# Pool projection ahead of the in-projection, its moving averages one per token tile inside the in-projection, memory keys and values behind it

## The chip, the cores and the metric

The kernel runs on one core of a Trainium2 chip. The core has a matmul engine (TensorE, PE in the profile; its weight loads are PEld), a vector engine (VectorE, DVE), an activation engine (ScalarE, ACT), a general engine (GpSimd, POOL) and a queue engine that mostly issues DMAs (SyncE, SP). Each engine works through its own instructions in order; semaphores tie them together. The metric is the time of one execution on the device in microseconds (us), the median of a few runs. Lower is better.

## The reference, cut to what matters

One layer, batch 1, 2048 tokens (S) of width 1024 (D), all in float32:

```python
xn = rmsnorm(h, g_mix)
z = einsum('bsd,dc->bsc', xn, w_in)            # q 512 | k 512 | v 512 | p_in 512 | f_logit 8
q, k = rmsnorm per head of 64 (8 heads)
fox  = forgetting_attention(q, k, v, f_logit + b_forget)   # causal, cumulated log-sigmoid of f_logit as bias
pool = multiscale_pool(p_in, w_pool, pool_scale)           # 4 groups of 128 channels: mean over the last
                                                           # 2, 4, 8, 16 tokens minus the token, a 128x128 map, a scale
h = h + concat(fox, pool) @ w_out
hn = rmsnorm(h, g_mem_q); mn = rmsnorm(mem, g_mem_kv)      # mem: 256 tokens
mq, mk, mv from hn @ w_mem_q and mn @ w_mem_kv             # 4 heads of 128
h = h + softmax(mq mk^T / sqrt(128)) mv @ w_mem_out
h = h + swiglu(rmsnorm(h, g_ffn))
```

## The kernel before, in words

Every float32 matmul of a projection is made of three: each operand is split into a rounded high part and the low rest, and `mm3` (lines 58 to 62) multiplies high by high, high by low and low by high. So wherever a tile of activations or weights enters a projection, ACT makes the high part (a copy or a scaled copy, lines 157, 176, 181) and DVE the low one (lines 55, 177), two instructions of the tile's size.

The part that the change touches lies ahead of the attention and takes 460 us. All of it but the last stage is written out by hand: each engine's instructions stand in the order in which the code issues them.

1. Memory keys and values (`kv`): 16 steps of weights for 256 memory tokens, 96 matmuls of 512 columns. The loads of the x tiles and of the in-projection's weights (`load_w_in`, 8 pieces of 128 x 1544) run under it.
2. In-projection: 16 tiles of 128 tokens. `project` multiplies a tile into four PSUM banks of 386 columns (tiles `zps`, one per quarter n, 96 matmuls), `scaled` copies the four banks out on ACT (line 327), `normed_heads` splits v, writes it to DRAM, and squares q and k (line 348); DVE sums the squares per head (line 350), POOL takes the power -1/2 (`rsqrt`, lines 69 and 71), and `split_heads` (lines 358 to 363 and 55) scales and splits q and k. `to_heads` (lines 372 to 375) turns them on PE, copies them on ACT and stores them. There are four PSUM banks for `zps`, so the first quarter of tile i+1 needs the copy of the first quarter of tile i. For each pair of tiles x is squared on ACT (line 160), added up on POOL (line 162) and summed over its channels on PE against ones (`token_sums`, line 202); this gives `rstd`, the norm of each token.
3. Pool projection: 8 blocks of 256 tokens, 96 matmuls each (`zp`), the transposed way round (channels on partitions, tokens along the row). The token norms are spread over the partitions by a matmul (`stat_diag`, `stat_bcast`, line 491). `windows` scales the block on DVE, builds the means by adding shifted copies (line 516), and splits the result; `pooled` multiplies it by `w_pool`. Under it `out_sums` prepares sums of the out-projection's weights on POOL, `cumulated` makes the cumulated forget logits (tiles fe, tots, car, written to DRAM as `cd`), and `load_head` loads the first head (`qs`, `kh`, `kl` from `qkT`, `cb` from `cd`).
4. Attention: 22 score items run ahead of the first value item. A score item is two matmuls (line 715) and one DVE instruction that adds the bias and takes the row minimum (line 717); the diagonal ones need a mask from POOL (`cm`, line 706).

Of the kernel before, what the change touches and what calls it, by code (L numbers as in the profile page):

```python
# [21 lines left out]
H = 8  # L22
# [18 lines left out]
def block_kernel(ctx: ExitStack, tc: tile.TileContext, x, xT, memT, cols, rows, w_qkvf, w_p, w_pool, w_out,  # L41
# [81 lines left out]

    xstack, lstack = ExitStack(), ExitStack()
    zp = opened(lstack, "zp")
    xp = opened(xstack, "xp", side="right")

    class Slots:
# [5 lines left out]
        def take(self, dt):  # L134
            n = self.free.pop(0)
            return n, self.pl.tile(self.shape, dt, tag=f"{self.name}{n}", name=f"{self.name}{n}", bufs=1)

# [14 lines left out]
    def x_split(tiles, part=None, qs=range(4), engs={}):  # L152

        for q in qs:
            n, raw = tiles[q]
            hi = xp.tile([P, 2, B], F32R, tag="xhi", name="xhi", bufs=8)
            act.copy(hi[:], raw[:])
            if part is not None:
                sq = xp.tile([P, 2, B], F32, tag="xsq", name="xsq", bufs=2)[:] if q else part
                act.activation(sq, raw[:], AF.Square, scale=1.0 / 32.0)  # L160
                if q:
                    pool.tensor_tensor(out=part, in0=part, in1=sq, op=ALU.add)
            m, lo = xsl.take(F32R)
            sub_hi(lo[:], raw[:], hi[:], engs.get(q))
            xsl.free.append(n)
            xlow.append(m)
            tiles[q] = hi, lo
# [18 lines left out]
    whi = [None] * KD  # L186
    wlo = [None] * KD
    wph = [None] * KD
    wpl = [None] * KD
    HIS = 16  # L190

    with ExitStack() as c0:
        was = ExitStack()
        wa = opened(was, "wa", side="right")
        tpp = opened(xstack, "tpp", space=PSUM)

        def token_sums(part):

            ssp = tpp.tile([P, 2], F32, tag="ss", name="ss", bufs=1)
            for j in range(2):  # L200
                for c in range(2):
                    pe.matmul(ssp[:, j:j + 1], lhsT=part[:, c, j * P:(j + 1) * P], rhs=ones[:, 0:1], start=c == 0,
                              stop=c == 1)
            return ssp

        def token_rstd(ssp, outp):
            ms = xp.tile([P, 2], F32, tag="ms", name="ms", bufs=2)
            dve.tensor_copy(ms[:], ssp[:])
            rsqrt(outp, ms[:])


        kvs = ExitStack()
        kvp = opened(kvs, "kvp", space=PSUM)
        first = in_order(EN.DVE, EN.Activation, EN.Pool, EN.SP)
        first.__enter__()
        kv = [[kvp.tile([P, MW], F32, name=f"kv{m}{a}") for a in range(2)] for m in range(2)]
        wk = [None] * KD
        wsl = Slots(wa, [P, QKVF], "wl", KD)
        w_raw = [None] * KD

        def w_in_hi(k, dt):

            return wa.tile([P, QKVF], dt, tag=f"wh{k}", name=f"wh{k}", bufs=1)

        def load_kv(k):
            wk[k] = w_in_hi(k, F32)[:, :2 * MW]
            sp.dma_start(wk[k], w_mem_kv[k * P:(k + 1) * P, :])

        def split_kv(k):
            t_ = slab(k % 3, dt=F32R)  # L230
            hi, lo = t_[:, :2 * MW], t_[:, 2 * MW:]
            split(hi, lo, wk[k], g_mem_kv[:, k:k + 1])
            return hi, lo

        def load_w_in(k):

            n, raw = wsl.take(F32) if k < KD - 1 else (None, slab(3))
            w_raw[k] = n, raw[:, :QKVF]
            sp.dma_start(w_raw[k][1], w_qkvf[k * P:(k + 1) * P, :])

        def split_w_in(k):
            n, raw = w_raw[k]
            whi[k] = w_in_hi(k, F32R)
            wlo[k] = wsl.take(F32R)[1]
            split(whi[k][:], wlo[k][:], raw, g_mix[:, k:k + 1])
            wsl.free.append(n)

        mt = []
        for k in range(4):
            mt += x_load(0, memT.rearrange("(k p) m -> p k m", p=P), (k,))  # L250
            load_kv(k)
        xt = x_load(0)
        mpart = xp.tile([P, 2, B], F32, tag="part", name="part", bufs=1)
        mr = cst.tile([P, 2], F32, name="mr")
        for k in range(KD):
            if k < 4:
                x_split(mt, mpart[:], (k,))
            wh, wl = split_kv(k)
            mh, ml = x_part(mt, k)
            if k == 3:  # L260
                token_rstd(token_sums(mpart), mr[:])
            for m in range(2):
                ms_ = slice(m * P, (m + 1) * P)
                for a in range(2):
                    as_ = slice(a * MW, (a + 1) * MW)
                    mm3(kv[m][a][:], (mh[:, ms_], ml[:, ms_]), (wh[:, as_], wl[:, as_]), k == 0, k == KD - 1)
            if k < 4:
                load_kv(k + 4)
            if k == 1:
                load_w_in(0)  # L270
            if k == 3:
                for c in range(1, KD):
                    load_w_in(c)
            if k == 6:
                split_w_in(0)
            if k == 5:
                part = xp.tile([P, 2, B], F32, tag="part", name="part", bufs=1)
                x_split(xt, part[:])
        split_w_in(1)
        mks_ = [slab(n, dt=F32R)[:].rearrange("p (a c) -> p a c", a=2) for n in (2, 0)]  # L280
        mkv = [t_[:, a] for t_ in mks_ for a in range(2)]
        mkh, mkl = (t_.rearrange("p (h m) -> p h m", h=MH) for t_ in mkv[:2])
        mvh, mvl = (t_.rearrange("p (m c) -> p m c", m=2) for t_ in mkv[2:])
        mks, msk = ([zp.tile([P, MH, P], F32, tag="st", name="mks", bufs=4) for _ in range(2)] for _ in range(2))
        for m in range(2):
            act.activation(mks[m][:].rearrange("p h d -> p (h d)"), kv[m][0][:], AF.Copy, scale=mr[:, m:m + 1])
            split_gain(mvh[:, m], mvl[:, m], kv[m][1][:], mr[:, m:m + 1])
        for n in range(2, 4):
            sp.dma_start(mkvd[n], f(mkv[n]))
        kvs.close()  # L290

        def mem_key_norms():
            for m in range(2):
                act.activation(msk[m][:], mks[m][:], AF.Square)
                ms = zp.tile([P, MH], F32, tag="mkms", name="mkms", bufs=2)
                dve.tensor_reduce(out=ms[:], in_=msk[m][:], axis=AX.X, op=ALU.add)
                rk = zp.tile([P, MH], F32, tag="mkr", name="mkr", bufs=2)
                rsqrt(rk[:], ms[:], 1.0 / P)
                dve.tensor_tensor(out=mks[m][:], in0=mks[m][:], in1=rk[:].unsqueeze(2).to_broadcast([P, MH, P]),
                                  op=ALU.mult)  # L300
# [1384 lines left out]
```

## Time and profile before

| | |
|---|---|
| median of 3 runs | 2590.38 us (2587.77 to 2593.8) |
| profiled execution, span from first to last instruction | 2586.7 us |
| granted TensorE clock, mean | 0.994 |
| PE busy in the span | 2522.3 us (98%) |
| DVE, ACT, POOL busy | 1740.9 (67%), 1286.9 (50%), 892.2 us (34%) |
| DMA | 416.13 MB, mean 161 GB/s |

The page does not give a time of its own for the profiled execution; its span is 3.7 us under the median of the runs, and what is worked out against the span is carried over to the median by adding these 3.7 us. In the rows, "idle before <-releaser" is how long the engine stood still ahead of an instruction and which instruction of which line ended that. The duration of a matmul overlaps its neighbours, so the pace of matmuls is read from start to start.

### The profile page before, as it was taken

Reading aid. Unit: us, or ns where it says so; the run is one execution under the profiler, and the core shown is the slowest. Engines: PE = TensorE matmul, PEld = TensorE weight load, DVE = VectorE, ACT = ScalarE, POOL = GpSimd, SP = SyncE. Lnnn points to the kernel's source line nnn. Section 1 sums busy time; section 2 is a strip of 40 time slices with the busy share of each in tenths; the row PEclk is TensorE's granted clock in tenths of the full one; section 3 lists DMA queues with packets and bytes.
Section 4 is the critical chain, followed back from the end, with each engine's and each line's share of the span. In section 5 each row is a group of like instructions: output and inputs, shape, how many; then the busy total and the mean of one; then the engine's idle time right before and its main releaser. Section 6 shows DMA issues by size and latency. Waiting matters only on the chain.

```text
span 2586.7 us, 37147 instructions
## 1 busy us (share of the span) xinstructions
PE 2522.3 (98%) x13037; PEld 2169.7 (84%) x13037; DVE 1740.9 (67%) x2955; ACT 1286.9 (50%) x2444; POOL 892.2 (34%) x1185
## 2 busy tenths in 40 slices
PE   8999989999999899999999999999999999999998
PEld 7999989788888687788878888888888888888887
DVE  6444477899998755545877778756766666665554
ACT  6454443788889523555643433334543333333443
POOL 3343255445555522344425545430001222222000
PEclk9999999999999999999999999999999999999999
DMA  6443476644543545122464545447773332325665
GB/s 242 127 131 106 127 220 213 175 123 123 152 121 95 171 161 212 70 87 89 177 215 179 187 171 195 147 159 268 247 261 123 113 112 102 127 98 181 230 215 184
DMA packets 223434, 416.13 MB, mean 161 GB/s; under 512 B 26128, under 2 KB 113936, under 8 KB 212496
## 3 DMA queue, kind: packets, MB, share of 16 engines
q1 hardware_dynamic: 190800, 307.84, 37.2%
q0 software_dynamic: 32448, 105.93, 10.6%
q8 instruction: 102, 1.67, 0.3%
q14 instruction: 84, 0.69, 0.1%
HBM read 280.39 MB, written 133.30 MB: 160 GB/s over the span
## 4 chain that ended last, share of the span: by engine, by line
PE 46%; issue 8%; DVE 2%; DMA 2%; ACT 1%; POOL 1%; SPq 0%; POOLq 0%; DVEq 0%; ACTq 0%
PE bk L60 13%; PE bk L62 13%; PE bk L61 13%; PE mmps L60 2%; PE mmps L62 2%; PE mmps L61 2%; PE tp L896 1%; DMA graw<-in_w_gu_dram 1%; DVE ww L55 1%; DVE t L991 0%; DMA xraw<-hTd 0%; POOL out_dram L1578 0%; ACT mq L1069 0%; DMA hTd<-hst 0%; DVE ms L1073 0%
## 5 line engine op out<-in xcount | busy, mean ns | idle before, releaser
L55 DVE TENSOR_TENSOR ww<-draw,ww 128x512 fp32r<-128x512 f32 x308 | 205.3, 703 | 156.5 <-ACT ww L181 155.8
L181 ACT CAST ww<-draw 128x512 fp32r<-128x512 f32 x308 | 179.4, 620 | 219.7 <-PE bk L62 179.2
L55 DVE TENSOR_TENSOR ww<-graw,ww 128x512 fp32r<-128x512 f32 x220 | 179.1, 821 | 107.4 <-ACT ww L181 107.0
L61 PE MATMUL bk<-ww,ww 128*128 128x512 f32 x616 | 239.9, 389 | 0.0
L62 PE MATMUL bk<-ww,ww 128*128 128x512 f32 x616 | 239.8, 389 | 0.0
L60 PE MATMUL bk<-ww,ww 128*128 128x512 f32 x616 | 239.8, 389 | 0.0
L181 ACT CAST ww<-graw 128x512 fp32r<-128x512 f32 x220 | 135.7, 621 | 181.5 <-PE bk L62 158.1
L55 DVE TENSOR_TENSOR pl<-tp,ph 128x512 fp32r<-128x512 f32 (+3 forms) x296 | 176.9, 599 | 27.5 <-ACT ph L809 25.4
L728 ACT ACTIVATE s<-s,mx 128x1024 f32<-128x1024 f32 (+2 forms) x192 | 173.7, 905 | 5.4 <-DVE mx L722 4.5
L793 PE MATMUL tp<-ident,s 128*128 128x128 f32 x1088 | 171.6, 274 | 4.7 <-DVE pl L55 4.3
L60 PE MATMUL zps<-wh,xhi 128*128 128x386 f32 x512 | 175.8, 343 | 0.1
L61 PE MATMUL zps<-wl,xhi 128*128 128x386 f32 x512 | 173.7, 339 | 0.0
L62 PE MATMUL zps<-wh,xl 128*128 128x386 f32 x512 | 173.4, 339 | 0.0
L809 ACT CAST ph<-tp 128x512 fp32r<-128x512 f32 (+3 forms) x296 | 148.5, 513 | 35.9 <-PE tp L793 30.3
L793 PEld LDWEIGHTS tp<-ident,s 128*128 128x128 f32 x1088 | 134.1, 141 | 32.5 <-DVE pl L55 7.7
L1578 POOL DMA_DIRECT2D out_dram<-o x32 | 17.3, 541 | 382.6 <-DVE o L1575 381.6
L62 PE MATMUL bk<-qs,ww 128*128 128x512 f32 x352 | 137.3, 390 | 1.0 <-DVE ww L55 1.0
L60 PE MATMUL bk<-qs,ww 128*128 128x512 f32 x352 | 138.0, 392 | 0.3 <-ACT s L1497 0.3
L61 PE MATMUL bk<-kh,ww 128*128 128x512 f32 x352 | 137.1, 389 | 0.0
L61 PE MATMUL bk<-cb,ww 128*128 128x512 f32 x352 | 137.0, 389 | 0.0
L60 PE MATMUL bk<-kl,ww 128*128 128x512 f32 x352 | 137.0, 389 | 0.0
L62 PE MATMUL bk<-kl,ww 128*128 128x512 f32 x352 | 137.0, 389 | 0.0
(607 smaller groups left out, 7373.4 us busy)
## 6 DMA issues: line engine op xcount, KB each, us to landing
graw<-in_w_gu_dram SPq DMA_DIRECT2D x44, 1024.0 KB, 5.4
draw<-in_w_down_dram SPq DMA_DIRECT2D x66, 256.0 KB, 4.4
xl<-in_xT_dram SPq DMA_DIRECT2D x64, 256.0 KB, 4.9
qkT<-st SPq DMA_DIRECT2D x64, 256.0 KB, 2.7
wdr<-in_w_down_dram SPq DMA_DIRECT2D x22, 512.0 KB, 4.3
vd<-cb SPq DMA_DIRECT2D x16, 512.0 KB, 3.3
qs<-qkT SPq DMA_DIRECT2D x8, 1024.0 KB, 6.8
kh<-qkT SPq DMA_DIRECT2D x16, 512.0 KB, 7.9
```

What stands on the lines that cost most here:

```text
L55: (eng or dve).tensor_tensor(out=lo, in0=src, in1=f(hi), op=ALU.subtract)
L60: pe.matmul(ps, lhsT=sh, rhs=mh, start=first, stop=False, skip_group_check=goes_on)
L61: pe.matmul(ps, lhsT=sh, rhs=ml, start=False, stop=False, skip_group_check=goes_on)
L62: pe.matmul(ps, lhsT=sl, rhs=mh, start=False, stop=last, skip_group_check=goes_on)
L181: act.copy(hi, raw)
L728: act.activation(s[:, sl], s[:, sl], AF.Exp, bias=ng, scale=-1.0, accum_out=l[:, q, g:g + 1])
L793: pe.transpose(tp[:, q * P:(q + 1) * P], unit["rows"][q][:, j * P:(j + 1) * P], ident[:])
L809: act.copy(ph[:, sl], tp[:, sl])
L896: pe.transpose(tp[:, e_], src[:, q + e_], ident[:])
L1578: pool.dma_start(out[rows_, cs], o)
```

## The change

The three stages ahead of the attention are put in another order, all under one order written by hand: pool projection, in-projection, memory keys and values. What goes with it:

- The pool projection's result, not yet scaled by the token norm, is copied out by ACT (`keep_p`) and stored in DRAM (`pd`), 8 blocks in 4 tensors of 512 tokens.
- The token norms come from x in its own layout: `load_rows` loads 128 tokens, `square_rows` squares them on ACT with a running sum (two instructions of 512 per tile), `row_stats` finishes four tiles on POOL and stores `rstdd`. The squares and sums of x in the in-projection, `token_sums` on PE and `stat_bcast` on PE are gone, but for the memory tokens.
- Inside the in-projection each token tile i gets one moving average: `window(g = i % 4, T = i // 4)` for one group of 128 channels over 512 tokens, read from `pd`, with the norms spread by a DMA. `pooled` follows one tile later (three matmuls of 512). `out_sums` runs there too, its subtractions on DVE and no longer on POOL.
- Memory keys and values come after the in-projection, in 16 steps `kv(n)`; only three of their weight tiles (`EARLY`) are loaded before the in-projection's weights give up their place. The steps of `cumulated` and the last heads stand between them; the first head is loaded after `cd` is stored, and `mkvd` is stored from POOL.
- Small working tiles share 14 slots (`Slot`).

The core of the diff:

```diff
-    def x_split(tiles, part=None, qs=range(4), engs={}):
+    def x_split(tiles, part=None, qs=range(4)):
...
+        def square_rows(i):
+            for a, s in enumerate(rows_in.pop(i)):
+                act.activation(s.v, s.v, AF.Square, scale=1.0 / 32.0, accum_out=msx2[:, i, a:a + 1])
+                s.free()
...
+        for b in range(1, NB):
+            hs, ls = x_parts(xt)
+            nxt_raw = x_load((b + 1) % NB)
+            load_w_in(b)
+            for s_ in stores:
+                s_()
+            zs = [zpp.tile([P, 2, B], F32, tag="z", name="zp", bufs=4) for _ in range(2)]
+            if b >= 2:
+                load_rows(b - 2)
+            project_p(hs, ls, zs, range(KD), (0, 1))
+            split_w_in(b - 1)
+            x_split(nxt_raw)
+            stores = [keep_p(b, zs, 0)]
+            project_p(hs, ls, zs, range(KD), (2, 3))
+            if b >= 2:
+                square_rows(b - 2)
+            stores.append(keep_p(b, zs, 1))
+            xt = nxt_raw
...
+        def window(g, T, s):
+            pT = s.t
+            tt(quad(pT[:, HIS:]), quad(pT[:, HIS:]), rbs[T].v.rearrange("p (t q) -> p q t", q=4), ALU.mult)
...
+            for st in range(g + 1):
+                sh = 1 << st
+                lead = 2 * sh - 1
+                nx = Slot()
+                tt(nx.t[:, lead:], cur.t[:, lead:], cur.t[:, lead - sh:HIS + TB - sh], ALU.add)
...
+            dve.scalar_tensor_tensor(out=mixed, in0=cur.t[:, HIS:], scalar=1.0 / (2 << g), in1=mixed,
+                                     op0=ALU.mult, op1=ALU.subtract)
...
+            mh, ml = Slot(F32R), Slot(F32R)
+            split(mh.v, ml.v, mixed)
...
+                zps = project(i, j, hs, ls, range(1))
+                if i > 1:
+                    to_heads(i - 2, zr, (3,))
+                if mx is not None:
+                    po = pooled((i - 1) % NG, (i - 1) // NG, mx)
+                zps.update(project(i, j, hs, ls, range(1, 4)))
+                if i > 0:
+                    zr = split_heads(*st_)
+                if po is not None:
+                    po()
+                mx = window(i % NG, i // NG, pts.pop(i))
+                if "sums" in jobs:
+                    out_sums(i - i // 3, jobs.pop("sums"))
+                if i < 10:
+                    square_rows(i + 6)
+                if i in (1, 5, 9):
+                    row_stats((i + 6) // 4)
+                if i >= 13:
+                    split_kv(i - 13)
+                z = scaled(i, zps)
+                if i > 0:
+                    to_heads(i - 1, zr, range(3))
+                st_ = normed_heads(i, z)
+                if j == 0:
+                    if b + 1 < NB:
+                        x_split(xt)
...
+        for n in range(EARLY, EARLY + 6):
+            load_kv(n)
+        cum = cumulated()
+        next(cum)
+        kv(0)
+        to_heads(NT - 2, zr, (3,))
+        next(cum)
+        kv(1)
...
+        split_kv(3)
+        split_kv(4)
+        next(cum)
+        zr = split_heads(*st_)
+        dve.tensor_copy(mms[:], ssp[:, :2])
+        rsqrt(mr[:], mms[:])
+        kv(2)
+        po = pooled(NG - 1, NTB - 1, mx)
+        po()
+        kv(3)
+        split_kv(5)
+        next(cum)
+        kv(4)
...
+        kv(7)
...
+        next(cum)
+        kv(8)
...
+        next(cum)
+        for n in range(10, 14):
+            kv(n)
+            split_kv(n + 2)
+        head0.extend(load_head(0, hpa))
```

ACT, one token tile of the in-projection, before: the four copies of the banks (`kh`, `qs`: the z of the tile), the turned heads, the v cast (L341), the squares (L348), a pool weight's split, and the cast of the scaled heads (L363).

```order
L327 ACTIVATE kh<-zps,rstd 128x386 x4
L374 COPY st<-tp 128x512 x3
L341 CAST cb<-kh 128x8x64
L348 ACTIVATE cb<-kh 128x1024
L176 ACTIVATE wph_2082<-wpr,colt 128x512
L374 COPY st<-tp 128x512
L363 CAST kl<-cb 128x16x64
L327 ACTIVATE qs<-zps,rstd 128x386 x4
```

The same stretch in the changed kernel (`jl` are slots, `ss` is the bank of `pooled`):

```order
L358 ACTIVATE kh<-zps,rstd 128x386 x4
L399 COPY st<-tp 128x512 x3
L366 CAST cb<-kh 128x8x64
L373 ACTIVATE cb<-kh 128x1024
L399 COPY st<-tp 128x512
L388 CAST kl<-cb 128x16x64
L465 ACTIVATE jl_3447<-ss,colt 128x512
L196 CAST jl_3540<-jl_3198 128x512
L358 ACTIVATE qs<-zps,rstd 128x386 x4
```

Between the cast of the heads and the next tile's bank copies there now stand the output copy of `pooled` (L465) and the split of the moving average (L196, which reads DVE's result); up to tile 9 the two squares with running sums (L283) follow them.

SP, the first head's load, before: `qs`, `kh` and `kl` stand among the x loads of the pool projection; `cd` and `cb` follow some twenty rows later, and a block of x loads and the values `v` come behind them.

```order
L475 DMA wr<-in_w_pool_dram 128x4x128
L459 DMA qs<-qkT_84 128x2048
L554 DMA wor<-in_w_out_dram 128x2x256
L148 DMA xl_3776<-in_xT_dram 128x2x256
L148 DMA xl_3778<-in_xT_dram 128x2x256
L148 DMA xl_3780<-in_xT_dram 128x2x256
L148 DMA xl_3782<-in_xT_dram 128x2x256
L554 DMA wor<-in_w_out_dram 128x2x256
L461 DMA kh<-qkT_86 64x2048
L462 DMA kl<-qkT_86 64x2048
```

SP at the same loads in the changed kernel (`kr` are memory weight tiles):

```order
L400 DMA qkT_87<-st 128x4x128
L537 DMA kr<-in_w_mem_kv_dram 128x512 x7
L526 DMA cd<-jl_4575 128x128
L213 DMA qs<-qkT_84 128x2048
L215 DMA kh<-qkT_86 64x2048
L216 DMA kl<-qkT_86 64x2048
L215 DMA kh<-qkT_86 64x2048
L216 DMA kl<-qkT_86 64x2048
L217 DMA cb<-cd 128x2048
L207 DMA v<-vd 128x2048
```

All loads of the first head now stand behind the store of `cd`, and that behind the last memory weights.

POOL, the last norms and the running totals of the forget logits in the changed kernel; the 15 additions (L517, in the code before L586) make `car`, for which the PE matmul `loc` waits:

```order
L69 TENSOR_SCALAR zms<-zms 128x16
L71 TENSOR_TENSOR zrq<-zms,mhalf 128x16
L501 AFFINE_SELECT jl_4575<-ones 128x128
L503 MEMSET jl_4576 128x128
L69 TENSOR_SCALAR mms<-mms 128x2
L71 TENSOR_TENSOR mr<-mms,mhalf 128x2
L466 DMA poolT_130<-jl_4637 128x512
L517 TENSOR_TENSOR jl_4576<-jl_4576,jl_4575 128x8 x15
L67 TENSOR_SCALAR mkms<-mkms 128x4
```

Before, these additions stood among the subtractions and stores of `out_sums`:

```order
L557 TENSOR_TENSOR wor<-wor 128x256
L563 DMA wo_t_132<-wor 128x256
L563 DMA wo_t_134<-wor 128x256
L586 TENSOR_TENSOR car<-car,tots 128x8 x15
L546 DMA poolT_127<-po 128x4x256 x2
L557 TENSOR_TENSOR wot<-wor 128x256
```

They moved from the middle of the pool projection to the memory keys and values, behind the memory tokens' norm `mr`.

More of the change, by code (lines that the diff above doesn't have):

```diff
@@ L563, in out_sums @@
                 pool.dma_start(osum[nm][:, k, cs], v)
+            for s in r:
+                s.free()
         def cumulated():
             HN = H * NT
-            cp = lambda n: pt.tile([P, HN], F32, name=n)
-            utri, e, mn = cp("utri"), cp("fe"), cp("fmin")
-            pool.affine_select(out=utri[:], in_=ones[:], pattern=[[1, P]], compare_op=ALU.is_ge, fill=0.0, base=0,
+            sa, sb = Slot(), Slot()
+            cp = [sa.t[:, n * HN:(n + 1) * HN] for n in range(4)] + [sb.t[:, :HN]]
@@ L637, in block_kernel @@
+        for m in range(2):
+            split_gain(mvh[:, m], mvl[:, m], kvb[1, m][:], mr[:, m:m + 1])
+        for n in range(2, 4):
+            pool.dma_start(mkvd[n], f(mkv[n][:]))
+        lstack.close()
+        hp = opened(hps, "hp")
+        v0 = load_values(0)
     LEAD, LAG = 22, 3
```

703 lines of the change are left out of this document (336 added, 367 removed).

## The prediction

> **What bounds the kernel now.** I read the page's busy table first: only PE work or PE's waits can count.
>
> ```profile
> PE 2522.3 (98%) x13037; PEld 2169.7 (84%) x13037; DVE 1740.9 (67%) x2955; ACT 1286.9 (50%) x2444; POOL 892.2 (34%) x1185
> ```
>
> Then busy time by stretch, for where PE stands still ahead of the attention:
>
> ```profile
> 0.00:20.00 20.00, 11.14 (x40) 8.62 (x40) 10.36 (x12) 10.67 (x14) 5.59 (x11) 1.00 0.89 314
> 300.00:400.00 100.00, 92.91 (x666) 90.65 (x665) 65.88 (x99) 42.04 (x73) 49.77 (x67) 0.97 0.73 215
> 400.00:500.00 100.00, 92.71 (x651) 84.23 (x650) 82.09 (x192) 52.31 (x111) 41.89 (x74) 0.97 0.56 176
> ```
>
> The columns are the stretch, busy PE, PEld, DVE, ACT, POOL, granted clock, DMA share, GB/s. 14.4 us of PE are idle in the last two, in the pool projection and the start of the attention; the in-projection ahead of it has none. The waits name what comes last:
>
> ```profile
> PE rb L491 <- DVE diag L484: 3.3, 1, 3.3
> PE rb L491 <- DVE fmin L594: 2.9, 1, 2.9
> ```
>
> Both stand in the pool projection, where DVE is late. An idle gap costs twice:
>
> ```profile
> 369.52 1.22 PE L491 MATMUL rb<-diag,ones 128*128 128x256 f32 x2 [3.27 <-DVE diag L484]
> ...
> 371.18 0.41 PE L60 MATMUL zp<-xhi,wph 128*128 128x256 f32 x1
> ...
> 375.42 0.28 PE L62 MATMUL zp<-xhi,wpl 128*128 128x256 f32 x1
> ...
> 467.10 0.50 PE L715 MATMUL sps<-kh,qs 128*128 128x512 f32 x1 [2.20 <-DVE mx L717]
> ...
> 468.30 0.63 PE L715 MATMUL sps<-kh,qs 128*128 128x512 f32 x1
> ```
>
> After the gap of 3.27 us the same matmul takes 0.41 instead of 0.28 us until 375.4, about 5.7 us at half pace: 2.6 us lost on top, and the gap of 2.20 us is followed by slow matmuls too. A gap of 2 to 3 us or more is therefore priced at itself plus 2.6 us.
>
> The Trainium skill ("TensorE: Matmul & The Clock Gate", section "HAM oscillation — how this bites in real kernels") warns of idle gaps above about 3.4 us only; the 2.20 us row disagrees, and the row decides. By the Trainium skill the slow stretches below (3.9 us) would drop out, and the time would be 2586 instead of 2590 us.
>
> **What PE is spared, and its pace.**
>
> ```profile
> 303.39 1.02 PE L202 MATMUL ss<-ones,part 128*128 128x1 f32 x8
> 304.28 0.43 PE L60 MATMUL zps<-wh,xhi 128*128 128x386 f32 x1
> ...
> 317.07 1.13 PE L372 MATMUL tp<-identr,kl 128*128 128x128 f32 x12
> 318.04 0.41 PE L60 MATMUL zps<-wh,xhi 128*128 128x386 f32 x1
> ...
> 337.21 0.35 PE L60 MATMUL zp<-xhi,wph 128*128 128x256 f32 x1
> ...
> 345.57 0.28 PE L62 MATMUL zp<-xhi,wpl 128*128 128x256 f32 x1
> ```
>
> One token sum takes 0.89 us from start to start, and 8 of 9 go: 7.1 us. The 8 matmul pairs that spread the norms go as well, some 0.45 us each: 3.6 us. So about 11 us of PE work vanish, and the 14 us of waits above lose their place. 72 matmuls of 386 columns take 12.79 us, so 96 take 17.05; twelve turns take 0.97, sixteen 1.27 us. 72 matmuls of 256 columns (the first and last are shown) run 0.117 us apart. `pooled` becomes three matmuls of 512 columns, 0.70 us, which is what its six of 256 cost. I follow the new program along the clock, to the fourth score item on DVE, behind which both programs are equal.
>
> **Start and pool projection.**
>
> ```profile
> 5.75 0.62 ACT L157 CAST xhi<-xl 128x512 fp32r<-128x512 f32 x1 [3.68 <-DMA xl<-in_memT_dram]
> ...
> 7.13 1.15 ACT L176 ACTIVATE qs<-wh,colt 128x1024 fp32r<-128x1024 f32 x1 [0.23 <-DMA wh<-in_w_mem_kv_dram]
> ```
>
> Before, PE starts when this second instruction ends, at 8.3 us. Now the first weight tile is half as large in load and split: PE starts between 7.0 (5.75 and two 512-wide instructions of 0.62) and 8.3; I take 7.2. 768 matmuls by 0.117 are 89.8 us, the slow clock at the start 2.4 (as after the gap above), the hand-over between blocks 0.5: the stage ends at 100. Its copies, splits and squares take 6 of ACT's 11.2 us per block, and 2.8 MB per block is 250 GB/s, below the 314 of the first stretch above; I cost them at nothing, and at up to 4 us if a block's x comes late.
>
> **In-projection.** PE needs per tile 17.05 + 1.27 + 0.82 (`pooled`, with its switches), 19.14 us; the first two tiles 34.9, in all 302.9. But the bank copies of tile i+1 now stand on ACT behind the split of the moving average, and that is the end of a chain over three engines which starts with the bank copies of tile i. PE's next tile waits for the first of them. The chain's rows, two tiles of the in-projection before:
>
> ```profile
> 282.06 1.09 ACT L348 ACTIVATE cb<-qs 128x1024 f32<-128x1024 f32 x1
> ...
> 295.63 1.52 ACT L327 ACTIVATE kh<-zps,rstd 128x386 f32<-128x386 f32 x3
> 298.01 0.58 ACT L327 ACTIVATE kh<-zps,rstd 128x386 f32<-128x386 f32 x1 [0.85 <-PE zps L62]
> ...
> 299.91 0.65 ACT L341 CAST cb<-kh 128x512 fp32r<-128x512 f32 x1
> 300.43 1.09 ACT L348 ACTIVATE cb<-kh 128x1024 f32<-128x1024 f32 x1
> ```
>
> ```profile
> 288.60 2.31 DVE L358 TENSOR_TENSOR cb<-qs,zrq 128x1024 f32<-128x1024 f32 x1 [1.10 <-POOL zrq L71]
> ...
> 306.17 1.23 DVE L358 TENSOR_TENSOR cb<-kh,zrq 128x1024 f32<-128x1024 f32 x1 [3.39 <-POOL zrq L71]
> ...
> 310.97 0.15 DVE L208 COPY ms<-ss 128x2 f32<-128x2 f32 x1
> ```
>
> Four bank copies without the wait are 1.44 us up to the fourth's start, and from there to the end of the squares 3.51 (298.01 to 301.52): 4.95. From there over DVE's sum and POOL's power to L358 4.65 in an odd tile (301.52 to 306.17) and 5.45 in an even one (283.15 to 288.60), where x is split beside it. From L358 over the heads' split to DVE being free 4.80. The window's rows:
>
> ```profile
> 453.15 0.69 DVE L507 TENSOR_TENSOR pT<-zp,rbs 128x512 f32<-128x512 f32 x1
> 453.87 0.73 DVE L516 TENSOR_TENSOR s<-pT 128x542 f32<-128x542 f32 x1
> 454.63 1.47 DVE L516 TENSOR_TENSOR s<-s 128x538 f32<-128x538 f32 x2
> ...
> 265.05 0.74 DVE L177 SCALAR_TENSOR_TENSOR wpl<-wpr,colt,wph 128x512 fp32r<-128x512 f32 x1
> ```
>
> ```profile
> 466.74 0.19 ACT L728 ACTIVATION_READ_ACCUMULATOR s<-s,mx 128x1 f32 x1
> ```
>
> Scaling 0.72, two small copies 0.2, g+1 additions of 0.745, the final difference 0.75 with gaps: 1.74 + 0.745 (g+1). Then ACT's split 0.52 (the pace of 299.91), and up to tile 9 two squares, each with such a read of the sum, 0.64 each. The chain is thus 18.7 (g=0), 20.2 (g=1), 20.2 (g=2), 21.7 us (g=3) with squares, 1.3 less without, 0.45 more in the first three and 0.5 with a memory weight in the last. Against 19.1, and with the 1.6 us by which ACT may be late before PE notices, the excess adds up to waits of 1.3, 1.5, 3.0 in tiles 1 to 3, 0.6, 1.0, 2.6 in 5 to 7, 0.6 in 9, 1.1 in 11: 11.7 us. If each step is 1 us shorter, 3.0; 1 us longer, 24.6. I take 11.7, since every term has its row; PE's last projection ends at 100 + 302.9 + 11.7 = 414.6. The two longest waits bring slow clock, mostly inside a chain that is late anyway: 1.3 more. POOL's additions of x, which doubled L358 at 288.60, are gone; the chain has that in it. By the shapes DMA per tile grows from 2.0 to 3.5 MB, 180 GB/s; every load is issued a tile ahead, and costs nothing unless SP stands for more than 7 us behind a slot.
>
> **Memory keys and values.**
>
> ```profile
> L586 POOL TENSOR_TENSOR car<-car,tots 128x8 f32<-128x8 f32 x15 | 7.2, 477 | 4.2 <-DVE tots L583 3.1
> ```
>
> ```profile
> 468.32 0.20 POOL L741 TENSOR_TENSOR li<-l 128x4 f32<-128x4 f32 x1 [0.69 <-ACT s L728]
> ```
>
> ```profile
> L577 ACT ACT_TABLE_LOAD x1 | 1.3, 1283 | 0.0
> ```
>
> ```profile
> poolT<-po POOLq DMA_DIRECT2D x8, 512.0 KB, 6.1
> ...
> kl<-qkT SPq DMA_DIRECT2D x4, 512.0 KB, 10.6
> cb<-cd SPq DMA_DIRECT2D x2, 1024.0 KB, 12.4
> ```
>
> PE's own work is 96 x 0.234 = 22.5 us and about 7 for turns, sums and the last `pooled`. Counted from the end of the last projection, ACT reaches the last tile's squares at 7.2; DVE's sum, Exp, the table load of 1.28 and Ln come first, so `kv(3)` has its split at 12.5, while PE is free at 9.5: 3 us, with slow clock 5.6. `kv(5)` waits for the last tile's heads (4.80 again) until 19.1, about 1 us. The 15 additions start near 21; at 0.48 each PE gets `loc` at 28.5, at 0.20 (an addition of four words, unhindered) at 24; I take 26, as DVE rests then, 1 us of wait. `cd` is copied on DVE behind two more splits and two products that wait for POOL, at 33; only then does SP start the first head, 4 MB. `kv(15)` ends near 40. By the rows `kl` lands at 33 + 10.6, `cb` between 43 and 49, and the last `mkvd` store from POOL, whose place the scores' buffers need, at 42.6 + 6.1. The mask follows: first score on DVE at 48.5, from 45 to 54.
>
> ```profile
> 466.35 0.69 DVE L717 CUSTOM_DVE_ANT_0 s<-sps,cm 128x512 f32<-128x512 f32 x1 [2.47 <-POOL cm L706]
> ```
>
> This is the fourth item before. **Sum:** 414.6 + 48.5 + 1.1 (three small items) = 464.2, plus 1.3: 465.5 against 466.35, so 0.9 us less than the span of 2586.7. With the 3.7 us by which the median of 2590.4 lies above that span: **2590 us, no change**. What PE saves is given back in waits.
>
> **The rivals.** *Faster:* the in-projection's chain fits. For it: the first steps overlap more than start-to-start times show, and each 0.5 us counts 16 times; against it: the order on ACT is fixed. With 1 us less per tile, 2590 - 8.7 = 2581. *Slower:* POOL holds DVE up inside the chain. Its DMA issues (five per tile) run beside the moving average; at 288.60 a POOL instruction beside it cost a DVE one 1.08 us. At that price per tile, 24.6 + 1 instead of 11.7: 2604. It decides from 0.4 us per tile on, where the sum passes 2595. Against it: those issues are not additions. *The norms are still summed on PE:* excluded, since the order of PE has one group of such sums left.
>
> **Chances.** This forecast 0.44, faster rival 0.27, slower 0.29. A change under 0.2% (5.2 us) cannot be told from none. The forecast's own range (start and load delays, 45 to 54 in the last stage) is 2582 to 2598: of it 0.15 faster, 0.55 same, 0.30 slower; 0.92 of each rival lies on its side. Faster 0.066 + 0.248 = 0.31, same 0.29, slower 0.40. The range runs from below the faster rival with an early end (2581 - 5) to the slower one: 2576 to 2605.
>
> **What would show it.** PE waits for ACT's bank copies at the start of tiles with g = 2 and 3, of 1 to 3 us, none from tile 12 on; a wait of about 3 us at `kv(3)`; the first score at 463. Wrong if the in-projection shows under 3 or over 20 us of waits, or if PE waits in the pool projection.

## The result, and the profile after

| | before | after |
|---|---|---|
| median | 2589.99 us (2587.77 to 2593.8, 4 runs) | 2624.07 us (2623.64 to 2624.57, 4 runs) |
| ratio, 95% interval | 1 | 1.0131, 1.0117 to 1.0146 |
| span of the profiled execution | 2586.7 us | 2622.9 us |
| granted clock, mean | 0.994 | 0.986 |
| fourth score item on DVE | 466.35 us | 496.87 us |

The change costs 34 us, where the prediction saw none. The spans of the two profiled executions lie 36.2 us apart. The fourth item comes 30.5 us later; another 4.4 us go in the out-projection, where PE's waits for `o` rise from 5.0 to 9.4 us; 1.3 us are not followed further.

The page's busy line of the kernel after:

```profile
PE 2520.4 (96%) x12909; PEld 2161.5 (82%) x12909; DVE 1736.9 (66%) x2995; ACT 1295.8 (49%) x2487; POOL 818.9 (31%) x1134
```

PE has 128 matmuls fewer, and its busy time hardly falls: part of the work now runs at a lower clock. The stretches of the kernel after (busy PE, PEld, DVE, ACT, POOL, granted clock, DMA share, GB/s) say where:

```profile
20.00:100.00 80.00, 80.00 (x669) 80.00 (x669) 31.55 (x35) 42.57 (x75) 1.49 (x3) 1.00 0.79 251
...
200.00:300.00 100.00, 94.18 (x562) 92.88 (x561) 59.02 (x86) 48.14 (x91) 28.97 (x30) 0.98 0.65 187
300.00:400.00 100.00, 98.58 (x597) 97.35 (x595) 61.06 (x86) 45.03 (x80) 26.48 (x26) 1.00 0.56 164
400.00:440.00 40.00, 27.27 (x158) 25.34 (x156) 23.88 (x31) 22.27 (x39) 13.83 (x10) 0.89 0.43 125
440.00:480.00 40.00, 27.81 (x111) 21.09 (x111) 14.94 (x24) 14.49 (x25) 11.06 (x26) 0.80 0.63 177
480.00:500.00 20.00, 6.12 (x18) 4.79 (x19) 4.01 (x17) 3.85 (x9) 3.90 (x14) 0.50 1.02 340
```

The pool projection stands without a gap. From 400 to 500 PE is busy for 61 of 100 us, part of it at half pace. In the last stretch PE works for 6 of 20 us, and only the DMA engines are full. PE's waits up to 540 us (total, times, longest):

```profile
PE sps L776 <- DVE mx L778: 14.0, 2, 13.8
PE ss L60 <- DVE mms L631: 10.0, 1, 10.0
PE zps L60 <- ACT kh L358: 8.7, 4, 3.6
...
PE sps L776 <- DMA kh<-qkT: 5.2, 1, 5.2
PE kv L60 <- ACT kh L358: 4.2, 1, 4.2
PE zps L60 <- ACT qs L358: 3.9, 2, 2.2
```

Two lines, `zps`, are the in-projection: 12.6 us. The other lines shown lie behind it. The last projection ends at 418.92 us, where the first of these rows of PE begins; the last row is the first of the two long waits, 10.04 us:

```profile
418.92 1.14 PE L397 MATMUL tp<-identr,kl 128*128 128x128 f32 x12
424.23 0.50 PE L60 MATMUL kv<-jl,xhi 128*128 128x512 f32 x1 [4.16 <-ACT kh L358]
...
441.47 0.80 PE L60 MATMUL ss<-jl,jl 128*128 128x512 f32 x1 [10.04 <-DVE mms L631]
```

At 441.47 PE wants the bank `ss` for the last pooled product. The bank still holds the memory tokens' sums, ready since 430, until DVE copies them (`mms`). What stands ahead of that copy on DVE:

```profile
435.00 1.42 DVE L192 SCALAR_TENSOR_TENSOR kw<-kr,colt,kw 128x512 fp32r<-128x512 f32 x2 [4.78 <-ACT kw L191]
...
436.54 1.22 DVE L383 TENSOR_TENSOR cb<-kh,zrq 128x1024 f32<-128x1024 f32 x1
...
440.12 1.22 DVE L55 TENSOR_TENSOR kl<-cb,kl 128x1024 fp32r<-128x1024 f32 x1 [1.11 <-ACT kl L388]
441.26 0.15 DVE L631 COPY mms<-ss 128x2 f32<-128x2 f32 x1
```

Two memory weights (late themselves: SP issued them at 428.76) and the whole split of the last heads. The second long wait is read on POOL and SP:

```profile
470.79 0.62 POOL L686 DMA_DIRECT2D mkvd<-mkv  x1 [7.65 <-ACT mkv L191]
...
474.20 0.53 POOL L690 DMA_DIRECT2D mkvd<-mkv  x1 [0.25 <-DVE mkv L192]
494.27 0.21 POOL L758 MEMSET l<- 128x8 f32 x4 [19.54 <-DMA mkvd<-mkv]
```

```profile
464.09 0.33 SPq L526 DMA_DIRECT2D cd<-jl  x1
464.46 0.43 SPq L213 DMA_DIRECT2D qs<-qkT  x1
...
467.70 0.53 SPq L217 DMA_DIRECT2D cb<-cd  x1
468.33 0.40 SPq L207 DMA_DIRECT2D v<-vd  x1
469.70 0.32 SPq L213 DMA_DIRECT2D qs<-qkT  x1
```

The first instruction of the attention on POOL clears a small tile `l` that lies on the place of the last `mkvd` tile. It waits 19.5 us until that tile's store has landed, and the masks, the scores on DVE and PE's next bank wait behind it. DVE's first and fourth score item:

```profile
495.15 0.29 DVE L778 CUSTOM_DVE_ANT_0 s<-sps,cm 128x128 f32<-128x128 f32 x1 [21.25 <-POOL cm L767]
...
496.87 0.69 DVE L778 CUSTOM_DVE_ANT_0 s<-sps,cm 128x512 f32<-128x512 f32 x1 [0.34 <-POOL cm L767]
```

In those 20 us the first head (4 MB), `v` (1 MB), the stores (2 MB) and the second head (4 MB) are all on their way.

### The profile page after: what moved, and what is told of

It is laid out like the page before. It is cut to its first block, busy times and chain, and to the rows that moved or that the text cites. A ratio compares the mean times of both kernels' runs of the same rounds, so it can differ in the third digit from the quotient of the medians.

```text
span 2622.9 us, 37103 instructions
## 1 busy us (share of the span) xinstructions
PE 2520.4 (96%) x12909; PEld 2161.5 (82%) x12909; DVE 1736.9 (66%) x2995; ACT 1295.8 (49%) x2487; POOL 818.9 (31%) x1134
## 4 chain that ended last, share of the span: by engine, by line
PE 45%; issue 8%; DVE 3%; DMA 2%; ACT 1%; POOL 1%; SPq 0%; POOLq 0%; DVEq 0%; ACTq 0%
PE bk L62 13%; PE bk L60 13%; PE bk L61 13%; PE mmps L62 2%; PE mmps L60 2%; PE mmps L61 2%; PE tp L957 1%; DVE ww L55 1%; DMA xraw<-hTd 0%; DVE t L1052 0%; DMA wqr<-in_w_mem_q_dram 0%; DMA graw<-in_w_gu_dram 0%; POOL out_dram L1639 0%; ACT mq L1130 0%; DMA hTd<-hst 0%
## 5 line engine op out<-in xcount | busy, mean ns | idle before, releaser
L196 ACT CAST ww<-draw 128x512 fp32r<-128x512 f32 x308 | 179.7, 620 | 216.9 <-PE bk L62 165.9
L196 ACT CAST ww<-graw 128x512 fp32r<-128x512 f32 x220 | 135.7, 621 | 181.5 <-PE bk L62 157.8
L60 PE MATMUL zps<-wh,xhi 128*128 128x386 f32 x512 | 175.5, 343 | 12.6 <-ACT kh L358 8.7
L776 PE MATMUL sps<-kh,qs 128*128 128x512 f32 (+2 forms) x320 | 129.5, 405 | 19.2 <-DVE mx L778 14.0
```

The costliest lines, as they stand in the source:

```text
L60: pe.matmul(ps, lhsT=sh, rhs=mh, start=first, stop=False, skip_group_check=goes_on)
L196: act.copy(hi, raw)
L776: pe.matmul(ps[:, :wn], lhsT=qs[:, i * P:(i + 1) * P], rhs=kk[:, 512 * c:512 * c + wn], start=(a == 0), stop=(a == 1))
```

## The experiments

Each starts from the changed kernel, some with several edits at once, and its time is to be read beside 2624.07 us (the run with the `mkvd` stores behind `cb` starts from the combined kernel). The spread of one kernel's runs is 1 to 8.5 us, so differences of 2 us are read from traces, not from medians.

### The memory sums copied first

```diff
         mms, mr = small([P, 2], "mms"), small([P, 2], "mr")
+        dve.tensor_copy(mms[:], ssp[:, :2])
+        rsqrt(mr[:], mms[:])
         split_kv(3)
         split_kv(4)
         next(cum)
         zr = split_heads(*st_)
-        dve.tensor_copy(mms[:], ssp[:, :2])
-        rsqrt(mr[:], mms[:])
```

> One step moved in the changed kernel: DVE copies the memory tokens' sums out of the one bank before it makes the lower parts of the memory weights 3 and 4, no longer behind those and the last tile's heads. Theory (the loss of 34 us sits behind the in-projection, and 10.0 us of it are this bank held): the last pooled product no longer waits for DVE mms; kv(3) then waits 2 to 3 us for its weights, whose split ended at 435.7; the rest of the stage runs 5.5 to 7 us earlier, and the time is 2617 to 2619. Rival 1 (the bank only covers weights that land late, or the loads behind it set the end anyway): 2622 to 2624. Rival 2 (the loss is in the in-projection's chain): no change.

Measured: 2621.89 us, 2.2 less, no more than the spread of its runs. The 10 us wait is gone, and PE's waits show what came in its place (ahead of the second row the ACT row that it waited for):

```profile
PE kv L60 <- ACT kw L191: 4.9, 2, 2.5
...
PE ss L514 <- ACT jl L465: 2.6, 1, 2.6
```

```profile
440.43 1.04 ACT L388 CAST kl<-cb 128x1024 fp32r<-128x1024 f32 x1 [3.42 <-DVE cb L385]
441.38 0.68 ACT L465 ACTIVATE jl<-ss,colt 128x512 f32<-128x512 f32 x1
```

The one bank went on to the pooled product, whose copy (L465) stands on ACT behind the cast of the last heads, and that behind the same two instructions of DVE. The theory named the holder of the bank, not all that waits in the row behind it; its 5.5 to 7 us were wrong.

### The place of mkvd

```diff
         kvp = opened(xstack, "kvp", side="right")
+        mkv = [kvp.tile([P, 1024], F32R, name=f"mkv{n}") for n in range(4)]
...
-        mkv = [kvp.tile([P, 1024], F32R, name=f"mkv{n}") for n in range(4)]
```

> The changed kernel with the four tiles that are stored as mkvd taken first from their pool instead of last, which moves their place in SBUF; no instruction moves. Theory (POOL's first memset, 19.5 us late, and the first scores stand on the place of the last mkvd tile until its store has landed): POOL no longer waits for a store, the first score follows the landing of cb at about 487.5 and stands on DVE at 488.5 instead of 495.15, 6.5 us less: 2617 to 2618. Rival (the loads of the first head, and not the place, set the start): no change, 2624.

Measured: 2611.27 us, 12.8 less. POOL:

```profile
472.65 0.53 POOL L690 DMA_DIRECT2D mkvd<-mkv  x1 [0.26 <-DVE mkv L192]
473.17 0.23 POOL L758 MEMSET l<- 128x8 f32 x4
483.40 2.27 POOL L767 TENSOR_SCALAR_AFFINE_SELECT cm<-cb 128x128 f32<-128x128 f32 x6 [10.00 <-DMA cb<-cd]
```

The memset no longer waits; the mask waits for `cb`, and the first score stands at 483.73 instead of 495.15. It gained 11.4 us instead of 6.5, since `cb` of the first head took 16.0 us to land; the expectation had used a median over both heads' `cb`. No instruction moved, only places in SBUF (the other tiles of this pool moved with the four): placing alone is worth 12.8 us here.

### The second head's loads later, twice

```diff
-                if b == 1 and h + 1 < H:
+                if b == (1 if h else 3) and h + 1 < H:
```

> The changed kernel with the second head's loads (4 MB) issued 20 score items later, behind the first store of the attention, so that they no longer share the DMA engines with the first head's loads and the mkvd stores. Theory (at 350 GB/s 4 MB are 12 us of transfer, and they delay cb and the last mkvd store): cb lands 10 to 13 us after its issue instead of 19.8, the last mkvd store by 486; the first score moves from 495 to 483 to 487, and the time is 2612 to 2616. Rival (the first head's and the stores' transfers are bound by their own queues): 2622 to 2625.

Measured: 2623.81 us, nothing. SP issued `qs`, half of `kh` and half of `kl` from 470.19 to 474.60 all the same, ahead of the last store of `mkvd`; only the 2 MB behind it had moved, and the store landed at 494.9 as before:

```profile
494.88 0.21 POOL L758 MEMSET l<- 128x8 f32 x4 [20.01 <-DMA mkvd<-mkv]
```

So the try was repeated with SP held to the order of the code:

```diff
-        with in_order(EN.DVE, EN.Activation):
+        with in_order(EN.DVE, EN.Activation, EN.SP):
```

> The earlier try moved only the second half of the second head's loads, which was issued behind the mkvd stores in any case; its first 2 MB (qs, kh, kl) stayed ahead of the last stores. Here SP keeps the order of the code in the attention, and all 4 MB of the second head stand behind the first store of the attention (ld). Theory (what is issued ahead of a transfer delays it, what is issued behind it does not): 2 MB fewer ahead of the last mkvd store are 5 to 7 us at 300 to 400 GB/s; the store lands at 487 to 490, the first score follows, 2616 to 2619. Rival (the four stores take their 20 us for themselves, or for the first head alone): last store at 494, 2622 to 2625.

Measured: 2621.86 us. With all 4 MB behind the last store, POOL waits less:

```profile
491.45 0.21 POOL L758 MEMSET l<- 128x8 f32 x4 [15.65 <-DMA mkvd<-mkv]
```

The last store took 16.1 us instead of 20.0, so the direction is right and the size, 4 us instead of 5 to 7, is not; 2.2 us of it show in the median, hardly more than the spread of its runs (1.9 us). The second head is the smaller part of the crowd.

### The first head's keys ahead of cd

```diff
         for n in range(EARLY + 6, 2 * KD):
             load_kv(n)
+        head0.extend(load_keys(0, hpa))
...
-        head0.extend(load_head(0, hpa))
+        head0.append(load_bias(0, hpa))
```

> The changed kernel with the first head's qs, kh and kl (3 MB) issued right behind the last memory weights, at about 456, no longer behind the store of cd at 464; cb stays behind cd. Theory (the first head, the mkvd stores, v and the second head together fill the DMA engines from 466 to 495, and the last mkvd store ends when they are through): 3 MB moved to where the engines are half idle shorten that by 7 to 9 us; PE's waits for kh and kl (7 us) go, the last store lands at 486 to 488, the first score moves by as much: 2615 to 2618. Rival (the mkvd stores are slow for their own queue, as moving half of the second head's loads did nothing): PE's waits for kh and kl go, but the first score stays: 2622 to 2625.

Measured: 2610.6 us, 13.5 less, more than expected. POOL's store and memset, then SP's `cd` and `cb`:

```profile
473.97 0.53 POOL L697 DMA_DIRECT2D mkvd<-mkv  x1 [0.25 <-DVE mkv L192]
481.79 0.21 POOL L765 MEMSET l<- 128x8 f32 x4 [7.29 <-DMA mkvd<-mkv]
```

```profile
465.06 0.34 SPq L532 DMA_DIRECT2D cd<-jl  x1
474.81 0.33 SPq L215 DMA_DIRECT2D cb<-cd  x1
```

The last store takes 7.7 us instead of 20: it was slow for what stood ahead of it. That is the 3 MB, and the second head too, which waits on SP behind `cb` and now starts at 476.6, behind the last store; by the try before, the second head's share of the 12 us is about 4. The 3 MB now stand ahead of `cd`, a store of 64 KB, and `cb` can only be issued 9.75 us after it, where 3.6 us lay between the two issues in the changed kernel.

### Three moves in the memory stage

```diff
+                if i == NT - 1:
+                    was.close()
+                    kvp = opened(xstack, "kvp", side="right")
+                    for n in range(EARLY, EARLY + 6):
+                        load_kv(n)
...
-        for n in range(EARLY, EARLY + 6):
-            load_kv(n)
...
-        zr = split_heads(*st_)
         kv(2)
         po = pooled(NG - 1, NTB - 1, mx)
         po()
+        zr = split_heads(*st_)
```

(and the copy of the sums first, as above)

> The changed kernel with three steps of the memory stage moved: the memory weights 3 to 8 are issued ahead of the last tile's stores (as soon as its projection frees their place), the memory sums are copied out of the one bank first, and the last pooled product and its copy stand ahead of the last tile's heads on ACT. Moving the second alone gained 2 us, since the bank went straight on to the pooled product, whose copy stood on ACT behind those heads. Theory (late weights and the one bank held by one step after the other keep PE 10 us): the waits for mms and for the bank's next copy go, kv(3) waits under 2 us, the last heads are turned 8 to 10 us earlier, and all behind moves by 7 to 9 us: 2614 to 2617. Rival (DVE's own chain for the last heads, late from the in-projection, sets it): 2 to 4 us, 2620 to 2622.

Measured: 2616.37 us, 7.7 less. The last matmul of `kv` starts at 464.30 instead of 472.01, and the first score stands at 488.04 instead of 495.15: what PE gains in the middle comes out at the end almost in full. Apart from the 4.2 us at `kv(0)`, the waits of PE that are left until the last `kv` step are short (the longest 3.5 us, for the next memory weights).

### The bank copies first

```diff
+                z = scaled(i, zps)
+                mx = mx()
                 if i < 10:
                     square_rows(i + 6)
...
-                z = scaled(i, zps)
```

`window` now ends with DVE's difference and returns the split as a function, which is called behind `scaled`.

> The changed kernel with ACT's copies of the four banks of tile i put ahead of the split of the moving average and of the squares of the rows. Theory: the 12.6 us that PE waits for these copies in the in-projection go, the wait of 4.2 us at kv(0) too or in part, and everything behind comes 11 to 14 us earlier: 2610 to 2613, with the 30 us lost behind the in-projection still there. Rival 1 (the in-projection's chain is the whole loss): 2590 or less. Rival 2 (the split that now stands later makes DVE or the last pooled product late instead): 2620 to 2626.

Measured: 2606.39 us, 17.7 less. The same stretch of the in-projection as above:

```profile
200.00:300.00 100.00, 99.89 (x604) 98.61 (x603) 63.79 (x93) 49.49 (x95) 34.00 (x35) 1.00 0.69 198
```

No wait is left and the clock is 1.00. The stage takes 300.7 us (101.44 to 402.14) instead of 317.2 (101.67 to 418.92): 12.6 us of waits and 3.9 us more. Of these, 2.8 us are slow matmuls in the changed kernel, behind its two longest waits (182.5 to 185.7 and 264.8 to 267.6 us). From the last projection to the first score it is 74.1 us, and was 76.2: the loss behind is almost untouched.

### Both, and all

The place of `mkvd` and the bank copies together:

> The place of mkvd apart and the bank copies first, together. Alone they gave 2611.3 and 2606.4. Theory (two losses one behind the other): the gains of 12.8 and 17.7 us add up to 2592 to 2595. Rival (both shorten the same wait): 2602 to 2606.

Measured: 2595.95 us, 28.1 less; the two gains alone add up to 30.5. So they are two losses, one behind the other. Then all edits that gained:

> All of these together: the bank copies first, the place of mkvd apart, the three moves in the memory stage, and the first head's qs, kh, kl ahead of cd. Theory (the 34 us are these waits, and the PE work that the change spares, 11 us, is then seen): the first projection's end moves from 419 to 406, the memory stage takes 42 to 46 us, cb lands before the last kv step ends, the first score stands on DVE at 447 to 453: 2576 to 2582, less than the kernel before. Rival (transfers at the start of the attention, or the order of ACT, bring new waits of 10 us): 2587 to 2594.

Measured: 2589.5 us, ratio to before 1.000 (0.999 to 1.0009). The last matmul of `kv` starts at 447.98 and the first score stands at 461.92. In between PE, DVE and ACT have next to nothing to do; SP's rows say why:

```profile
436.38 0.46 SPq L223 DMA_DIRECT2D kl<-qkT  x1
441.28 0.34 SPq L536 DMA_DIRECT2D cd<-jl  x1
453.56 0.33 SPq L215 DMA_DIRECT2D cb<-cd  x1
```

The store of 64 KB, issued behind 3 MB of loads on the same queue, takes 12.2 us to land; in the changed kernel, where it stands ahead of those loads, it took 1.5 us. This is the rival's price, and a transfer as it said. So `cd` was sent from POOL, the last memory weights were issued earlier, and `split_kv(5)` was put ahead of the last heads (against the changed kernel, cut to these lines):

```diff
-            sp.dma_start(cd[:], mn)
+            pool.dma_start(cd[:], mn)
...
+        split_kv(5)
+        zr = split_heads(*st_)
         kv(3)
-        split_kv(5)
...
-        to_heads(NT - 1, zr, range(4))
-        kv(6)
         for n in range(EARLY + 6, 2 * KD):
             load_kv(n)
+        to_heads(NT - 1, zr, range(4))
+        head0.extend(load_keys(0, hpa))
+        kv(6)
```

> The kernel that joined all moves gave 2589.5: its first score stood at 461.9, 12 us behind the last kv step, since the store of cd was issued at 441.3 behind 3 MB of loads of the first head on the same queue and cb could only be issued at 453.6. Here POOL issues the store of cd, the memory weights 9 to 15 are issued ahead of the last heads' stores, and the weights 5 are split ahead of the last heads. Theory (what is left of the loss is this transfer, not work): cd lands some 3 us after its issue, cb 5 to 8 us later, the first score stands on DVE at 447 to 452, and the time is 2575 to 2581, 8 to 14 us less than the kernel before. Rival (the DMA engines are full from 430 to 460 whatever the queue): 2585 to 2590.

Measured: 2580.55 us, ratio to before 0.9968 (0.9956 to 0.9981): faster than both kernels, 8.5 us less than before (2589.1 us in the runs beside it). The page's busy line, and the issues of `cd` on POOL and `cb` on SP:

```profile
PE 2511.8 (97%) x12909; PEld 2155.3 (84%) x12909; DVE 1737.4 (67%) x2995; ACT 1295.3 (50%) x2487; POOL 820.4 (32%) x1135
```

```profile
434.72 0.62 POOL L536 DMA_DIRECT2D cd<-jl  x1 [1.22 <-DVE jl L535]
```

```profile
443.55 0.34 SPq L215 DMA_DIRECT2D cb<-cd  x1
```

PE is busy for 10.5 us less than before (all stages together, slow clock included), which fits the 11 us of work that the change spares. But `cd` did not land in 3 us from the other queue; 8.8 us lie between the issues. The Trainium skill ("DMA: Bandwidth & Descriptors", section "Issuing engines are not separate DMA queues") says that transfers of all issuing engines run on the same 16 DMA engines and interleave. These rows agree: from POOL's queue the small store still takes 8.8 us, with 3 MB of loads issued on SP in the 5 us ahead of it. How much of the step from 12.3 to 8.8 us between the issues is the queue's is not shown, since the loads were moved as well. The last try put the `mkvd` stores behind `cb`:

```diff
-            pool.dma_start(mkvd[n], f(mkv[n][:]))
+            sp.dma_start(mkvd[n], f(mkv[n][:]))
```

> The combined kernel of 2580.6 us, with the mkvd stores issued from SP behind cb instead of from POOL ahead of it. There the first score stood at 452.1 on DVE, since cb was issued at 443.6 and landed at 451.6, behind 2 MB of stores. Theory (again, what is issued ahead delays): cb lands 3 to 5 us earlier, the first score stands at 447 to 449, 2576 to 2579. Rival (the first head's own loads and cd set it, or the stores now hold SP): 2580 to 2584.

Measured: 2581.32 us (2579.48 to 2587.38), ratio 0.9979 (0.997 to 0.9988). The first score stands at 449.86 instead of 452.12, and the time does not fall. The rival's time came true; which of its two reasons holds is not shown.

### Without POOL's additions

```diff
-                if q:
-                    pool.tensor_tensor(out=part.v, in0=part.v, in1=sq, op=ALU.add)
```

> The changed kernel without POOL's three additions of the squared memory tokens (it leaves out three quarters of their sum of squares, so the memory keys' and values' scale is wrong). Theory: these additions, 5.8 us on POOL from 410.6 on, double the two instructions of DVE beside them (2.32 and 2.20 us instead of 1.22), and DVE's chain of the last tiles is on the path: DVE takes 1.22 us for both, PE's wait at kv(0) falls from 4.2 to about 2 us, the time by 2 us to 2621 to 2623. Rival (DVE's slower pace there has other causes, such as POOL's DMA issues): the two stay at 2.2 us, 2624.

Measured: 2622.05 us, 2 less, within the spread of its runs; PE's wait at `kv(0)` falls from 4.2 to 2.1 us. The two instructions of DVE, first in the changed kernel, then without the additions:

```profile
410.61 2.32 DVE L383 TENSOR_TENSOR cb<-qs,zrq 128x1024 f32<-128x1024 f32 x1 [1.12 <-POOL zrq L71]
412.97 2.20 DVE L385 TENSOR_TENSOR cb<-cb,gqs 128x1024 f32<-128x1024 f32 x1
```

```profile
410.22 1.23 DVE L381 TENSOR_TENSOR cb<-qs,zrq 128x1024 f32<-128x1024 f32 x1 [1.12 <-POOL zrq L71]
411.48 1.23 DVE L383 TENSOR_TENSOR cb<-cb,gqs 128x1024 f32<-128x1024 f32 x1
```

Beside them stood POOL's three additions, 5.76 us from 410.56 on. They cost DVE 2.1 us. The Trainium skill ("SBUF — State Buffer", section "SBUF: two separate sides") describes a pair of ports that an instruction of GpSimd and one of VectorE with two SBUF inputs can hold only one at a time; these rows agree.

## Why the prediction was wrong, step by step

**Start and pool projection: right.** The in-projection starts at 101.7 us; the step said 100, and PE does not wait in the pool projection.

**The work that PE is spared: right.** 11 us were worked out; the busy time of the combined kernel, where most waits are gone, is 10.5 us lower.

**The in-projection's chain: right, its slow clock too small.** Predicted were 11.7 us of waits for ACT's bank copies, behind the windows with many additions. Measured are 12.6: at the starts of tiles 3, 4, 7, 8 and 12, behind the windows with g = 2 and 3 (1.7, 3.3, 2.2, 3.6 and 1.4 us), and 0.4 at tile 2; none later in this stage. The chain reached one step further than the prediction said: `kv(0)` waits 4.2 us for the bank copies of the last tile, also behind a window with g = 3. Beside the waits 3.9 us were lost, 2.8 of them to slow matmuls, and the step had 1.3; the work itself took 300.7, and the step had 302.9. The last projection ends at 418.9 instead of 414.6. The price of an idle gap, itself plus 2.6 us from 2 to 3 us on, did not hold as a rule: behind 2.23 us the matmuls kept their pace, behind 3.60 us they lost 1.3 us and behind 3.27 us 1.5.

```profile
242.05 0.44 PE L60 MATMUL zps<-wh,xhi 128*128 128x386 f32 x1 [2.23 <-ACT qs L358]
242.33 0.34 PE L61 MATMUL zps<-wl,xhi 128*128 128x386 f32 x1
...
265.64 0.53 PE L62 MATMUL zps<-wh,xl 128*128 128x386 f32 x1
```

**The rival "POOL holds DVE": slower, but not for its reason.** It asked for more than 24 us of waits in the in-projection. The measured 12.6 us leave no room for it. POOL's additions do double DVE's instructions, but at one place, for 2.1 us; the price of its DMA issues was not tried by itself.

**Memory keys and values: here it failed.** The step said that the first score stands on DVE 48.5 us after the last projection, 45 to 54. It stood there after 76.2. Its parts, from the end of the last projection:

| | predicted | measured |
|---|---|---|
| `kv(0)` waits for the bank copies | none | 4.2 us |
| wait ahead of `kv(3)` | 3 us | 10.0 us (bank `ss`) |
| `cd` is issued | 33 us | 45.2 us |
| last `kv` step ends | 40 us | 53.5 us |
| last `mkvd` store, issue to landing | 6.1 us | 20.0 us |
| first score | 48.5 us | 76.2 us |

Two errors of about the same size make the 27.7 us. The first, 13 us, is the stage's own chain. The prediction followed ACT and DVE to `kv(3)`, but gave the sums, the last pooled product and the totals no bank: it did not see that all share one, and that each is released by an engine that stands behind the last heads. The three moves took 7.7 us of it back. It had no term for the loads of the memory weights either: SP issued the last seven of them only at 451.82, behind the stores of the last heads; ACT waited for them, and PE behind ACT for 2.8 us:

```profile
456.45 0.72 ACT L191 ACTIVATE kw<-kr,colt 128x512 fp32r<-128x512 f32 x1 [4.92 <-DMA kr<-in_w_mem_kv_dram]
```

In the combined kernel, where these loads come earlier, ACT does not wait for them, and the last `kv` step ends 37.3 us after the last projection (404.33 to 441.59), under the 40 of the step.

The second, 14 us, is one duration. The step took 6.1 us for the store from a row of the program before, the median of eight stores that took 3.5 to 14.4 us there. It named the wait (the scores' buffers need the place), and `cb` and the store were both in it, but it did not count the bytes. The two stretches of the kernel after in which the store was on its way (the last two columns are DMA share and GB/s):

```profile
470.00:480.00 10.00, 2.95 (x12) 1.91 (x10) 2.80 (x4) 1.87 (x3) 2.21 (x4) 0.80 1.01 239
480.00:490.00 10.00, 1.62 (x5) 1.14 (x5) 0.00 (x0) 0.00 (x0) 0.00 (x0) 0.50 1.01 423
```

11 MB are asked for between 464 and 480 us, and at the 423 GB/s of the fullest stretch they take 27 us. That is a lower end: between 470 and 480 us the engines were just as full and moved 239 GB/s, for a reason that stays open. Taking the place away (12.8 us) and loading the keys earlier (13.5 us) show it in two ways.

**The sum.** Against the predicted 465.5 us the fourth item stands 31.4 later: 4.3 from the last projection, 27.7 from the memory stage and 0.6 from the items between, less the 1.3 that stood as a term of its own. The span is 37.1 us over the predicted one; 4.4 of the rest are PE's waits for `o` in the out-projection, which were 5.0 us before and 6.8 to 10.1 us in all kernels with the change. Why they grew stays open, as do the last 1.3 us. The median lies 1.2 us over the span, where 3.7 were added; this makes 34.6 of the 37.1, or 34 against the rounded forecast.

**The faster rival** did not hold: the chain does not fit as it is written. Where it fits (the bank copies first), 16.5 us go with it; the rival had 8.7, since it left 3 us of waits and no clock to win.

## What to carry to other kernels

When a stage is moved to just ahead of another, count the bytes that both then ask for in that stretch and divide by what the DMA engines moved at their fullest: this is a lower end. The median landing of a like transfer in another stage can be far off (here 6.1 us for 20.0). For each shared bank and each place in SBUF, write down who takes it, who gives it back, and what stands ahead of that one on its engine: a wait that is removed goes to the next in that row. And a small store that others wait for (here 64 KB) belongs ahead of large loads, not behind them.

## What the runs showed of the hardware

- One and the same 512 KB store took 7.7, 16.1 and 20.0 us to land, by the number of bytes issued ahead of it. Moving 2 MB that were issued behind it changed nothing.
- With the same busy share (1.01) the DMA engines moved 239 GB/s in one stretch of 10 us and 423 in the next.
- Behind a wait of PE of 2.77 us (at 457.2) the matmuls ran at full pace first; the slow ones (0.63 us instead of 0.39) began 1.6 us later and lasted until 465.5, with shorter waits between them. Behind the wait of 10.04 us they were slow at once, until 445. In the in-projection the waits of 3.27 and 3.60 us were followed by some 3 us of slow matmuls each, those of 2.23 us and less by none.
